# A decoder trunk on one core: the order of value products, the layout of the compression inputs, and a projection tile of 32 features

## The chip, the cores and the metric

The program runs on one core of one Trainium2 chip. The metric is the device time of one execution in microseconds (us). Engines: PE is the matrix engine (PEld its weight loads), DVE, ACT and POOL work on tiles, SP issues the DMAs. All five run their own instruction lists in order and wait for each other by semaphores.

## The reference

Two layers work on a stream x of 512 tokens by 1024 features. Layer 0 mixes tokens by sparse attention, layer 1 by an RWKV-7 recurrence; each adds attention into 256 memory tokens, an output projection and a gated FFN. All is float32. Three places matter here:

```
# layer 0, compression of keys and of values (kv: 512 tokens x 4 groups x 64)
idx = arange(31)[:, None] * 16 + arange(32)[None, :]
blocks = kv[:, idx] + pos                      # 31 blocks of 32 tokens, 16 apart
hid = gelu(einsum('bnlgd,lde->bnge', blocks, w1))   # w1: 32 places x 64 x 128
# layer 0, selected and window branch, per group of 3 heads
o_s = einsum('bgrqk,bgqkd->bqgrd', p_s, vg)    # probabilities times values, 64 wide
o_w = einsum('bgrqk,bkgd->bqgrd', p_w, vwc)
# memory attention, per head: p (512 x 256) times v (256 x 64)
# layer 1: one projection h @ w_in, of which the gate input has 160 columns
r, k, v, zw, za, zg = split(z, [768] * 3 + [64, 64, 160])
```

## The kernel before

Features lie on the 128 partitions and the 512 tokens along the row. A projection (`gemm`) makes a tile of 128 features: its weights are loaded as eight blocks of 128x128, and weights (`wsp`) and inputs (`nxh`/`nxl`, `wxh`/`wxl`, ...) are each split into a high and a low part, so a block takes three products in one PSUM tile `pm`: high by high, high by low, low by high (`mm3`). That makes 24 products of 512 columns a tile.

The program is first recorded as a list of operations (`Rec.add`). A planner (`Rec.schedule`) then sets the order: it steps through time with a cost per operation (`cost`), lets each engine take the ready operation that stands first in the recorded list (plus a bias for the projections that serve as filling), and keeps bounds on tiles alive. A matrix product that uses a part of the array (`colmode`) is joined to others of the same mode where one is ready. The order it finds is each engine's instruction list; the chip then keeps it. Every instruction is issued from line 517, so the profile tells them apart by tiles only.

The places that the change touches:

- **Attention of layer 0** (`nsa`): per group g of 3 heads and tile qt of 128 queries, probabilities `p` of two branches are transposed on PE (`ptr`), copied to `ap` by ACT or DVE, and multiplied with the values `vst`. The product of a branch is 64 wide: branch 0 writes partitions 0 to 63 of `po`, branch 1 partitions 64 to 127 (`tile_position=(0, 64 * br)`). There are 80 such products of 384 columns (float32, which is two PE instructions each). The memory attention (`mem_attn`, four times) does the same with its two heads, `mpt` and `mvs`, 512 columns, in `pa`.
- **Compression** (`compress`, once for keys, once for values): two projections give `kcf` (128 features, 512 tokens); SP copies them by DMA into `kc2`, 64 partitions at a time, the upper half shifted by one token. Then 16 float32 products with the weights `cw1` take every 16th column, 129 of them (32 blocks x 4 groups, and one column of the position vector `cpos`). The buffer `kc2` exists once.
- **Layer 1** (`rwkv`): tile 20 of the input projection holds the last 32 columns of the gate input, padded with zeros to 128, and is computed like every other tile. Only rows 0 to 31 of its result (`zg2`) are read.

Of the kernel before, what the change touches and what calls it, by code (L numbers as in the profile page):

```python
# [11 lines left out]
F32 = mybir.dt.float32  # L12
F32R = mybir.dt.float32r
F16 = mybir.dt.float16
AF = mybir.ActivationFunctionType
ALU = mybir.AluOpType
# [545 lines left out]
def cost(eng, meth, args, kw, outs, ins):  # L562

    def size(v):
        return int(np.prod(v.shape[1:])) if len(v.shape) > 1 else 1
    if meth == "dma_start":
        v = (outs + ins)[0]
        return v.shape[0] * size(v) * 4 / 350.0, 0
    n = max(size(v) for v in outs)
    ps = any(v.t.tag[1] for v in outs[:1] + ins)  # L570
    if eng == "tensor":
        if meth == "transpose":
            dt, m = ins[0].dt, outs[0].shape[0]
            return (0.85 if dt == F32 else 0.45) * size(ins[1]) * 1.0 + 2, 158
        w, x = ins[0], ins[1]
        m, n = w.shape[-1] if len(w.shape) == 2 else size(w), size(x)
        if x.dt == F32:
            t = n * 4 / 2.4 + 5
            if n == 129:
                t *= 2  # L580
            if m <= 64 and w.shape[0] <= 64:
                t = 58.0 if n <= 64 else 55.0
            elif n <= 64 and m <= 64:
                t = 54.0 if m > 32 else 27.0
            elif n >= 256 and m == 64:
                t = n * 2 / 2.4 + 5
            elif n < 128:
                t = max(t, 215.0 if m > 64 else 112.0 if m > 32 else 60.0)
        elif x.dt == F32R:
            t = n / 2.4 + 13  # L590
        else:
            t = n / 2.4 + 2 if m > 64 else 16
        return t, 158
    if eng == "vector":
        cols = [v for k, v in kw.items() if k.startswith("scalar") and isinstance(v, AV)]
        t = 67 + 61 * bool(cols)
        if meth == "reciprocal":
            return 67 + n * 8 / 1.2, 92
        if meth in ("tensor_reduce", "tensor_tensor_reduce"):
            n = size(ins[0])  # L600
            return t + n / 0.96 + 12, 92
        fast = meth in ("tensor_copy", "tensor_scalar", "memset") and not ps
        if meth == "tensor_tensor" and all(v.dt == F16 for v in outs + ins):
            fast = True
        return t + n / (1.92 if fast else 0.96), 92
    if eng == "scalar":
        t = (51 if ps else 93) + n * 0.833
        if isinstance(kw.get("scale"), AV):
            t += 93
        if "accum_out" in kw:  # L610
            t += 145
        return t, 110
    if meth == "tensor_tensor":
        return 150 + 2.1 * n, 40
    if meth == "memset":
        return 60 + 0.75 * n, 60
    return 250 + 0.77 * n, 40


class B:  # L620
# [203 lines left out]
                                                          scalar2=None, op0=ALU.mult)))  # L824

    def copied(self, out, ps):
        self.nc.flex(("scalar", "copy", (out, ps), {}), ("vector", "tensor_copy", (out, ps), {}))

    def kdup(self, kf, half, kh, kl):

# [18 lines left out]
    def mem_attn(self, m, qm, kv, ot):  # L849

        nc = self.nc
        kh, kl, vs = kv
        qs = [self.qstack(qm, i, "mqs") for i in range(2)]
        prs = []
        for qt in range(4):
            ps = self.ax_ps()
            tok = slice(qt * 128, qt * 128 + 128)
            for i in range(2):
                h = 2 * m + i
                o = ps[:, 256 * i:256 * i + 256]  # L860
                nc.tensor.matmul(o, qs[i][:, tok], kh[h], start=True, stop=False)
                nc.tensor.matmul(o, qs[i][:, tok], kl[h], start=False, stop=True)
            mn = self.sm("mmn", [128, 2], bufs=4)
            nc.vector.tensor_reduce(out=mn, in_=ps.rearrange("p (i n) -> p i n", i=2),
                                    op=ALU.min, axis=AX.X)
            sm = self.sm("msm", [128, 2], bufs=4)
            p = self.s2("mp")
            for i in range(2):
                nc.scalar.activation(p[:, 256 * i:256 * i + 256], ps[:, 256 * i:256 * i + 256],
                                     AF.Exp, bias=mn[:, i:i + 1], scale=-1.0,  # L870
                                     accum_out=sm[:, i:i + 1])
            rs = self.sm("mrs", [128, 2], bufs=4)
            nc.vector.reciprocal(out=rs, in_=sm)
            for i in range(2):
                nc.gpsimd.tensor_scalar(out=p[:, 256 * i:256 * i + 256],
                                        in0=p[:, 256 * i:256 * i + 256],
                                        scalar1=rs[:, i:i + 1], scalar2=1.0,
                                        op0=ALU.mult, op1=ALU.mult)
            prs.append(p)
        po = self.ax_ps()  # L880
        for mt in range(2):
            pts = []
            for i in range(2):
                pt = self.ax_ps()
                for qt in range(4):
                    nc.tensor.transpose(pt[:, qt * 128:qt * 128 + 128],
                                        prs[qt][:, 256 * i + 128 * mt:256 * i + 128 * mt + 128],
                                        self.ident)
                pts.append(self.s2("mpt"))
                self.copied(pts[i], pt)  # L890

            for i in range(2):
                nc.tensor.matmul(po[64 * i:64 * i + 64], vs[mt][:, 2 * m + i], pts[i],
                                 start=mt == 0, stop=mt == 1, tile_position=(0, 64 * i))
        self.copied(ot[6 + m], po)


# [64 lines left out]
    def nsa(self, xt):  # L962
# [37 lines left out]
        def compress(kvis):  # L1000

            for kvi in kvis:


                flat = nc.tile([128, 2080], F32, "kc2", "kc2", 1)
                kc2 = flat[:, 0:2048].rearrange("p (g n) -> p g n", g=4)
                cpos = self.sm("cpos", [128, 16])
                nc.sync.dma_start(cpos, self.a["cpos"][kvi])
                nc.gpsimd.tensor_scalar(out=flat[:, 2048:2080:2], in0=cpos, scalar1=1.0,
                                        scalar2=1.0, op0=ALU.mult, op1=ALU.mult)  # L1010
                for m in range(2):
                    with self.fill(GB[0]):
                        ps = self.gemm(W[2 * kvi + m], xs)
                    kcf = self.s2("kcf")
                    nc.vector.tensor_tensor(out=kcf, in0=ps, in1=R, op=ALU.mult)
                    for half in range(2):
                        hs = slice(64 * half, 64 * half + 64)
                        g = 2 * m + half
                        nc.sync.dma_start(kc2[0:64, g, :], kcf[hs])
                        nc.sync.dma_start(kc2[64:128, g, 0:511], kcf[hs, 1:512])  # L1020
                ps = self.ax_ps()
                for c in range(2):
                    cw = self.wraw(self.a["cw1"][kvi][:, c * 1024:c * 1024 + 1024])
                    for l in range(8):
                        ll = 8 * c + l
                        w = cw[:, l * 128:l * 128 + 128]
                        nc.tensor.matmul(ps[:, :129], w, flat[:, 2 * ll:2 * ll + 2049:16],
                                         start=ll == 0, stop=ll == 15)
                pb = self.sm("cpb", [128, 1])
                nc.vector.tensor_copy(pb, ps[:, 128:129])  # L1030
# [148 lines left out]
        for g in range(G):  # L1179
# [15 lines left out]
            for qt in range(4):  # L1195
# [8 lines left out]
                for br in range(2):  # L1204
# [21 lines left out]
                    for r in range(3):  # L1226
# [1 line left out]
                        nc.gpsimd.tensor_scalar(out=p, in0=p, scalar1=rs3[:, r:r + 1],  # L1228
                                                scalar2=gate[:, qt, gc:gc + 1],
                                                op0=ALU.mult, op1=ALU.mult)  # L1230
                aps = []
                for kt in range(qt + 1):
                    for br in range(2):
                        pt = self.ax_ps("ptr", F32, (128, 384))
# [1 line left out]
                            nc.tensor.transpose(pt[:, r * 128:r * 128 + 128],  # L1236
                                                pbr[br][r][:, kt * 128:kt * 128 + 128], self.ident)
                        aps.append(self.s2("ap")[:, :384])
                        self.copied(aps[-1], pt)

                for kt in range(qt + 1):
                    for br in range(2):
                        nc.tensor.matmul(po[64 * br:64 * br + 64], vst[kt][:, br, g],
                                         aps[2 * kt + br], start=kt == 0, stop=kt == qt,
                                         tile_position=(0, 64 * br))
                for m2 in sorted({(3 * g + r) // 2 for r in range(3)}):
                    if ot[m2] is None:
                        ot[m2] = self.s2("ot")
# [12 lines left out]
        return ot  # L1261


    def rwkv(self, xt):
        nc = self.nc
        xs = [self.split(xt[k], "wx", self.v("n1_1", k)) for k in range(KT)]
# [8 lines left out]
            return proj(wa, ma, na), proj(wb, mb, nb)  # L1275

        def proj_(wi, mix, name):
            ps = self.gemm(W[wi], xs)
            z = self.s2(name)
            if mix is None:  # L1280
                nc.vector.scalar_tensor_tensor(out=z, in0=ps, scalar=-0.125, in1=R,
                                               op0=ALU.mult, op1=ALU.mult)
                return z
            nc.vector.tensor_tensor(out=z, in0=ps, in1=R, op=ALU.mult)

            d = self.s2("zd")
            nc.scalar.activation(d, z, AF.Copy, scale=omu[:, mix:mix + 1])
            nc.vector.scalar_tensor_tensor(out=d[:, 1:512], in0=z[:, 0:511],
                                           scalar=self.v("mu", mix), in1=d[:, 1:512],
                                           op0=ALU.mult, op1=ALU.add)  # L1290
            return d

# [539 lines left out]
```

## Time and profile before

| | |
|---|---|
| median of 3 runs | 1453.22 us (1451.1 to 1454.13) |
| the profiled execution | 1453.28 us, its span 1451.5 us |
| PE busy | 1418.1 us, 98% of the span |
| PE at full clock | 0.993 of it on average |
| DVE / ACT / POOL busy | 57% / 45% / 9% |
| DMA | 28.5% of the engines' time on the one queue, 92 GB/s |

A busy time counts from the start of an instruction to its modelled end, and ends overlap the next starts on PE. What a PE instruction costs is therefore read as the distance from its start to the next start. In a timeline row with a count (x16) the first start stands in front, and the next row's start says when the group let go.

### The profile page before, as it was taken

How to read it: one execution, taken by the hardware profiler on the slowest of the kernel's cores; microseconds unless marked ns; L12 is line 12 of the kernel's file. 1: busy time of each engine (PE TensorE's matmuls, PEld its weight loads, DVE VectorE, ACT ScalarE, POOL GpSimd, SP SyncE). 2: the span in 40 equal slices, each digit the busy share in tenths (PEclk: the TensorE clock that was granted, in tenths of full speed). 3: DMA queues.
4: the chain of work that ended last, by engine and by line, in shares of the span. 5: the costliest groups of instructions: out<-in, count | busy, mean ns of one | idle time of the engine just before them, and what ended most of it. 6: DMA issues, size and time to landing. Idle time of an engine off the chain costs nothing.

```text
span 1451.5 us, 24917 instructions
## 1 busy us (share of the span) xinstructions
PE 1418.1 (98%) x9914; PEld 1131.7 (78%) x9914; DVE 834.2 (57%) x1735; ACT 656.4 (45%) x1443; POOL 125.8 (9%) x214
## 2 busy tenths in 40 slices
PE   9999999999999999999999999999899999999997
PEld 7867776778888888888777777866688888888886
DVE  7754478756444544544559968786474444434435
ACT  7654477644223432333546565684452323312314
POOL 0232125310000000000000010210000000000003
PEclk9999999999999999999999999999999999999998
DMA  7333522232233323223213011012232333322212
GB/s 251 109 83 102 154 65 80 96 109 91 80 120 102 122 96 102 93 97 115 97 62 103 24 54 53 12 50 89 75 102 80 109 102 101 101 89 86 88 58 74
DMA packets 50228, 133.39 MB, mean 92 GB/s; under 512 B 6208, under 2 KB 14784, under 8 KB 50112
## 3 DMA queue, kind: packets, MB, share of 16 engines
q1 hardware_dynamic: 50112, 131.80, 28.5%
q8 instruction: 78, 1.28, 0.4%
q14 instruction: 38, 0.31, 0.1%
HBM read 122.34 MB, written 4.19 MB: 87 GB/s over the span
## 4 chain that ended last, share of the span: by engine, by line
PE 87%; DVE 4%; ACT 3%; DMA 2%; issue 1%; POOL 1%; SPq 0%; ACTq 0%; POOLq 0%; DVEq 0%
PE pm L517 68%; PE pa L517 13%; PE po L517 2%; PE pv L517 2%; PE ptr L517 2%; PE py L517 1%; DVE gram L517 1%; POOL p L517 1%; ACT tm L517 1%; DMA bias<-bias 0%; PE pg L517 0%; ACT gyo L517 0%; SPq L517 0%; POOL mp L517 0%; ACT p L517 0%
## 5 line engine op out<-in xcount | busy, mean ns | idle before, releaser
L517 PE MATMUL pm<-fxh,wsp 128*128 128x512 f32 x1408 | 435.1, 389 | 0.0
L517 DVE TENSOR_TENSOR wsp<-wraw,wsp 128x512 fp32r<-128x512 f32 (+2 forms) x432 | 280.8, 663 | 63.7 <-ACT wsp L517 61.7
L517 PEld LDWEIGHTS pm<-fxh,wsp 128*128 128x128 f32 x1408 | 264.1, 188 | 54.7
L517 ACT CAST wsp<-wraw 128x512 fp32r<-128x512 f32 (+2 forms) x432 | 238.6, 592 | 96.7 <-DMA wraw<-w_fi 66.2
L517 PE MATMUL pm<-fxl,wsp 128*128 128x512 f32 x704 | 274.0, 389 | 0.0
L517 PE MATMUL pm<-hxh,wsp 128*128 128x512 f32 (+1 forms) x736 | 220.4, 380 | 0.0
L517 PEld LDWEIGHTS pm<-hxh,wsp 128*128 128x128 f32 x736 | 136.3, 188 | 26.2
L517 PEld LDWEIGHTS pm<-fxl,wsp 128*128 128x128 f32 x704 | 132.1, 188 | 27.4
L517 PE MATMUL pm<-hxl,wsp 128*128 128x512 f32 (+1 forms) x368 | 139.4, 380 | 0.0
L517 DVE TENSOR_TENSOR xt<-pm,xt 128x512 f32<-128x512 f32 (+1 forms) x80 | 50.4, 637 | 133.5 <-PE pm L517 133.3
L517 PE MATMUL pm<-wxh,wsp 128*128 128x512 f32 x368 | 126.1, 408 | 0.0
L517 ACT CAST hxh<-hu 128x512 fp32r<-128x512 f32 x44 | 27.3, 621 | 207.6 <-DVE hu L517 207.6
L517 DVE TENSOR_TENSOR hu<-pm,R 128x512 f32<-128x512 f32 x44 | 30.4, 692 | 121.6 <-PE pm L517 121.6
L517 ACT ACTIVATE hg<-hg 128x512 f32<-128x512 f32 x44 | 27.8, 632 | 153.4 <-DVE hg L517 153.4
L517 PE MATMUL pm<-oxh,wsp 128*128 128x512 f32 x256 | 86.8, 411 | 1.2 <-ACT mp L517 0.7
L517 PE MATMUL pm<-nxh,wsp 128*128 128x512 f32 x256 | 86.4, 405 | 1.6 <-ACT nxh L517 1.1
L517 POOL TENSOR_SCALAR p<-p,ars,gate 128x128 f32<-128x128 f32 (+3 forms) x96 | 72.0, 765 | 173.8 <-DVE ars L517 107.3
L517 PEld LDWEIGHTS pm<-wxh,wsp 128*128 128x128 f32 x368 | 67.4, 188 | 18.5 <-issue 5.8
L517 PEld LDWEIGHTS pm<-hxl,wsp 128*128 128x128 f32 x368 | 69.2, 188 | 13.1
L517 DVE TENSOR_TENSOR hg<-pm,R 128x512 f32<-128x512 f32 x44 | 30.4, 692 | 80.4 <-PE pm L517 75.5
L517 PE MATMUL pm<-wxl,wsp 128*128 128x512 f32 x184 | 74.6, 405 | 0.0
L517 ACT ACTIVATE p<-p,amn 128x128 f32<-128x128 f32 (+3 forms) x96 | 53.4, 559 | 19.4 <-DVE amn L517 18.9
(313 smaller groups left out, 2104.8 us busy)
## 6 DMA issues: line engine op xcount, KB each, us to landing
wraw<-w_fi SPq DMA_DIRECT2D x88, 512.0 KB, 3.3
wraw<-w_fo SPq DMA_DIRECT2D x24, 512.0 KB, 3.3
wraw<-w_rw SPq DMA_DIRECT2D x23, 512.0 KB, 3.4
wraw<-w_fo SPq DMA_DIRECT2D x24, 384.0 KB, 3.0
wraw<-w_o SPq DMA_DIRECT2D x16, 512.0 KB, 3.3
wraw<-w_nsa SPq DMA_DIRECT2D x12, 512.0 KB, 3.7
xt<-xT SPq DMA_DIRECT2D x16, 256.0 KB, 5.1
bias<-bias SPq DMA_DIRECT2D x12, 256.0 KB, 4.6
```

Source lines behind the costliest of these rows:

```text
L517: o.ret = getattr(getattr(nc, o.eng), o.meth)(*[res(x) for x in o.args], **{k: res(v) for k, v in o.kw.items()})
```

## The change

Three parts:

- **Value products in pairs.** `copied` returns its operation, and the product of each half names, for the planner alone, the copies of both halves as things to come after (`after=done`). No instruction is added.
- **Compression inputs by place.** `kc2` is now laid out as 8 places by 132 columns per partition: place l of a stride of 16 tokens, with odd and even tokens on the two partition halves, so that a product reads 130 neighbouring columns. The multiplication that makes `kcf` writes it sorted by place, reading `pm` and `R` 16 columns apart. A DMA moves 64 partitions with 8 pieces of 32 numbers each. POOL zeroes two columns and copies the positions in two steps. The planner's price for a product of 129 columns goes.
- **The 32-feature tile.** `narrow` copies the low parts of the 32 weight columns beside the high ones (ACT, two copies), so that one weight block holds both; two products a block are enough, 16 instead of 24. The result's rows 32 to 63 are then added to rows 0 to 31 (one ACT copy, one DVE addition), and what follows works on 32 partitions.

```diff
@@ cost
-            if n == 129:
-                t *= 2
@@ copied
-        self.nc.flex(("scalar", "copy", (out, ps), {}), ("vector", "tensor_copy", (out, ps), {}))
+        return self.nc.flex(("scalar", "copy", (out, ps), {}), ("vector", "tensor_copy", (out, ps), {}))
@@ mem_attn (nsa alike, with done[2 * kt:2 * kt + 2])
-                self.copied(pts[i], pt)
+                done.append(self.copied(pts[i], pt))
...
-                                 start=mt == 0, stop=mt == 1, tile_position=(0, 64 * i))
+                                 start=mt == 0, stop=mt == 1, tile_position=(0, 64 * i),
+                                 after=done)
@@ compress
-                flat = nc.tile([128, 2080], F32, "kc2", "kc2", 1)
-                kc2 = flat[:, 0:2048].rearrange("p (g n) -> p g n", g=4)
+                kc2 = nc.tile([128, 8, 132], F32, "kc2", "kc2", 1)
...
-                    nc.vector.tensor_tensor(out=kcf, in0=ps, in1=R, op=ALU.mult)
+                    k4 = kcf.rearrange("p (j e n) -> p j e n", j=8, e=2)
+                    def by_place(t):
+                        return t.rearrange("p (n j e) -> p j e n", j=8, e=2)
+                    nc.vector.tensor_tensor(out=k4, in0=by_place(ps), in1=by_place(R), op=ALU.mult)
...
-                        nc.sync.dma_start(kc2[0:64, g, :], kcf[hs])
-                        nc.sync.dma_start(kc2[64:128, g, 0:511], kcf[hs, 1:512])
+                        for e in range(2):
+                            nc.sync.dma_start(kc2[64 * e:64 * e + 64, :, 32 * g:32 * g + 32],
+                                              k4[hs, :, e, :])
...
-                        nc.tensor.matmul(ps[:, :129], w, flat[:, 2 * ll:2 * ll + 2049:16],
+                        nc.tensor.matmul(ps[:, :130], w, kc2[:, l, c:c + 130],
@@ new, for tile 20
+    def narrow(self, src, xs):
+        ps = self.mm_ps()
+        for c, (wh, wl) in enumerate(self.wload(src)):
+            w3, l3 = (w.rearrange("p (k n) -> p k n", k=4) for w in (wh, wl))
+            nc.scalar.copy(w3[:, :, 32:64], l3[:, :, 0:32])
+            for kk in range(4):
+                k, w = 4 * c + kk, wh[:, 128 * kk:128 * kk + 128]
+                nc.tensor.matmul(ps, w, xs[k][0], start=k == 0, stop=False)
+                nc.tensor.matmul(ps, w, xs[k][1], start=False, stop=k == KT - 1)
+        z = self.s2("zn")
+        nc.scalar.copy(z[0:32], ps[32:64])
+        nc.vector.tensor_tensor(out=z[0:32], in0=ps[0:32], in1=z[0:32], op=ALU.add)
```

How the order moves, in three places. PE, the first memory attention of layer 0 (`mpt` are its transposed probabilities; one row is one product, two PE instructions); before:

```order
L517 MATMUL pa<-cf,mp 128x128 x2
L517 MATMUL pa<-mpt,mvs 64x512
L517 MATMUL pa<-kl,qs 128x256
L517 MATMUL pa<-kh,qs 128x384
L517 MATMUL pa<-mpt,mvs 64x512 x3
L517 MATMUL ptr<-cf,p 128x128 x6
```

and of the changed program:

```order
L517 MATMUL pa<-kh,qs 128x384
L517 MATMUL pa<-kl,qs 128x384
L517 MATMUL pa<-kh,qs 128x384
L517 MATMUL pa<-kl,qs 128x384
L517 MATMUL pa<-mpt,mvs 64x512 x4
L517 MATMUL ptr<-cf,p 128x128 x6
```

One product stood alone and three in a row; now four stand in a row, the halves in turn.

PE, ahead of the products of the first compression (`kc` and a number is its input buffer), before:

```order
L517 MATMUL po<-ap,vst 64x384 x3
L517 MATMUL pm<-nxh,wsp 128x512
L517 MATMUL pm<-nxl,wsp 128x512
L517 MATMUL pm<-nxh,wsp 128x512 x2
L517 MATMUL pm<-nxl,wsp 128x512
L517 MATMUL pm<-nxh,wsp 128x512 x2
L517 MATMUL ptr<-cf,p 128x128 x3
L517 MATMUL pm<-nxl,wsp 128x512
L517 MATMUL ptr<-cf,p 128x128 x3
L517 MATMUL pm<-nxh,wsp 128x512
L517 MATMUL ptr<-cf,p 128x128
L517 MATMUL pa<-kc_1118,wraw 128x129 x16
```

and of the changed program:

```order
L517 MATMUL pa<-kh,qs 128x384
L517 MATMUL pa<-kl,qs 128x384
L517 MATMUL pa<-kh,qs 128x384
L517 MATMUL pa<-kl,qs 128x384
L517 MATMUL po<-ap,vst 64x384 x4
L517 MATMUL pm<-nxh,wsp 128x512
L517 MATMUL pa<-kc_67,wraw 128x130 x16
```

In both programs the last product of the projection that feeds `kcf` stands ahead of twelve products `pa<-kh,qs` and `pa<-kl,qs` of 384 columns, of which the four ahead of `po` are the last. Between it and the compression stand 31 products and transposes before, 17 after; at the second compression it is 34 before and 23 after, the first 23 alike.

SP, the DMAs of the second compression (`w_mk` and `w_mv` are weights of 512 KB each), before:

```order
L517 DMA kc_1604<-kcf 64x511
L517 DMA wraw<-w_mk 128x1024
L517 DMA kc_1604<-kcf 64x512
L517 DMA kc_1604<-kcf 64x511
L517 DMA wraw<-w_mv 128x1024
L517 DMA kc_1604<-kcf 64x512
L517 DMA kc_1604<-kcf 64x511
L517 DMA wraw<-w_mv 128x1024
```

and of the changed program:

```order
L517 DMA wraw<-w_mk 128x1024
L517 DMA kc_1584<-kcf 64x8x32 x4
L517 DMA wraw<-w_mk 128x1024
L517 DMA kc_1584<-kcf 64x8x32 x4
L517 DMA wraw<-w_mv 128x1024 x2
```

The last four copies now stand ahead of both loads of `w_mv`; before, one load stood among them.

## Rows read from the trace of the kernel before

**Rows 1.** The page: the span and the busy times (us, share of the span, instructions).

```profile
span 1451.5 us, 24917 instructions
...
PE 1418.1 (98%) x9914; PEld 1131.7 (78%) x9914; DVE 834.2 (57%) x1735; ACT 656.4 (45%) x1443; POOL 125.8 (9%) x214
```

**Rows 2.** Busy times in the stretch that holds layer 0's attention (stretch and its length in us, busy us and instructions of PE, PEld, DVE, ACT and POOL, PE clock, DMA share, GB/s).

```profile
0.00:290.00 290.00, 278.10 (x1540) 212.69 (x1540) 189.53 (x529) 185.70 (x493) 80.26 (x120) 1.00 0.39 118
```

**Rows 3.** What PE waited for (us in total, times, longest).

```profile
PE ptr L517 <- POOL p L517: 4.6, 5, 1.6
...
PE pa L517 <- DMA kc<-kcf: 0.8, 1, 0.8
```

**Rows 4.** PE's timeline at the two groups of compression products (start us, us, engine line op, out<-in, shape, count, idle time before and who ended it).

```profile
125.67 7.20 PE L517 MATMUL pa<-kc,wraw 128*128 128x129 f32 x32
132.70 1.38 PE L517 MATMUL ptr<-cf,p 128*128 128x128 f32 x11
...
161.97 7.26 PE L517 MATMUL pa<-kc,wraw 128*128 128x129 f32 x32 [0.84 <-DMA kc<-kcf]
168.88 0.82 PE L517 MATMUL pm<-nxh,wsp 128*128 128x512 f32 x2
```

**Rows 5.** PE's timeline at float32 products of 128 neighbouring columns (the sum of squares of the first norm).

```profile
28.21 1.05 PE L517 MATMUL pa<-cf,sq 128*128 128x128 f32 x8
29.02 0.48 PE L517 MATMUL pm<-nxh,wsp 128*128 128x512 f32 x1
```

**Rows 6.** PE's timeline at three groups of attention value products, each with the row after it, and the row ahead of the second and of it the next start.

```profile
82.34 4.08 PE L517 MATMUL po<-ap,vst 128*64 128x384 f32 x18
86.35 0.50 PE L517 MATMUL pa<-kh,qs 128*128 128x512 f32 x1
...
96.72 0.39 PE L517 MATMUL pm<-nxh,wsp 128*128 128x512 f32 x1
97.03 2.80 PE L517 MATMUL po<-ap,vst 128*64 128x384 f32 x16
99.77 0.50 PE L517 MATMUL pm<-nxh,wsp 128*128 128x512 f32 x1
...
189.11 0.86 PE L517 MATMUL po<-ap,vst 128*64 128x384 f32 x2
189.90 0.33 PE L517 MATMUL ptr<-cf,p 128*128 128x128 f32 x1
```

**Rows 7.** PE's timeline at the first memory attention's value products.

```profile
252.90 1.07 PE L517 MATMUL pa<-mpt,mvs 128*64 128x512 f32 x2
253.90 0.38 PE L517 MATMUL pa<-kl,qs 128*128 128x256 f32 x1
...
254.39 1.93 PE L517 MATMUL pa<-mpt,mvs 128*64 128x512 f32 x6
256.25 0.87 PE L517 MATMUL ptr<-cf,p 128*128 128x128 f32 x6
```

**Rows 8.** PE's timeline in layer 1's projections around tile 20: two rows between whose starts 24 products of 512 columns, as many as a tile has, were issued.

```profile
702.40 0.39 PE L517 MATMUL pm<-wxl,wsp 128*128 128x512 f32 x1
...
707.84 0.39 PE L517 MATMUL pm<-wxl,wsp 128*128 128x512 f32 x1
```

**Rows 9.** The timeline of all engines ahead of the first compression: the last product of its projection, the multiplication that makes `kcf`, the four DMAs, and what PE did meanwhile.

```profile
118.85 0.39 PE L517 MATMUL pm<-nxh,wsp 128*128 128x512 f32 x1
...
119.35 0.69 DVE L517 TENSOR_TENSOR kcf<-pm,R 128x512 f32<-128x512 f32 x1 [4.62 <-PE pm L517]
...
120.07 2.39 SPq L517 DMA_DIRECT2D kc<-kcf  x4
...
121.28 1.50 PE L517 MATMUL po<-ap,vst 128*64 128x384 f32 x6
...
122.71 0.50 PE L517 MATMUL pm<-nxh,wsp 128*128 128x512 f32 x1
...
123.05 0.40 PE L517 MATMUL pm<-nxl,wsp 128*128 128x512 f32 x1
```

**Rows 10.** The instructions that write or read `kcf` (duration in ns, least, median and most), and the time of their DMAs to landing.

```profile
L517 SPq DMA_DIRECT2D kc<-kcf x16: 461/594/957, 112.1 to 157.9; - x16
...
DMA to landing us min/median/max: 2.2/2.3/4.1
```

**Rows 11.** PE's timeline ahead of the second compression: the last product of its projection (first of the two), and the start at which 23 more had been issued.

```profile
154.37 0.71 PE L517 MATMUL pm<-nxh,wsp 128*128 128x512 f32 x2
...
158.57 0.27 PE L517 MATMUL ptr<-cf,p 128*128 128x128 f32 x1
```

**Rows 12.** SP's timeline there: a load of weights, and the last two copies of `kcf` behind it.

```profile
156.81 0.53 SPq L517 DMA_DIRECT2D wraw<-w_mv  x1
157.38 1.10 SPq L517 DMA_DIRECT2D kc<-kcf  x2
```

**Rows 13.** DMA issues (count, KB each, median us from issue to landing), and the page's row of the queue (packets, MB, share of 16 engines' span).

```profile
out<-xout SPq DMA_DIRECT2D x8, 256.0 KB, 2.4
...
kc<-kcf SPq DMA_DIRECT2D x8, 128.0 KB, 2.3
mkh<-mkh SPq DMA_DIRECT2D x16, 64.0 KB, 1.9
...
q1 hardware_dynamic: 50112, 131.80, 28.5%
```

More of the change, by code (lines that the diff above doesn't have):

```diff
@@ L881, in mem_attn @@
         for mt in range(2):
-            pts = []
+            pts, done = [], []
             for i in range(2):
@@ L1002, in compress @@
             for kvi in kvis:
-                flat = nc.tile([128, 2080], F32, "kc2", "kc2", 1)
-                kc2 = flat[:, 0:2048].rearrange("p (g n) -> p g n", g=4)
+                kc2 = nc.tile([128, 8, 132], F32, "kc2", "kc2", 1)
                 cpos = self.sm("cpos", [128, 16])
                 nc.sync.dma_start(cpos, self.a["cpos"][kvi])
-                nc.gpsimd.tensor_scalar(out=flat[:, 2048:2080:2], in0=cpos, scalar1=1.0,
-                                        scalar2=1.0, op0=ALU.mult, op1=ALU.mult)
+                nc.gpsimd.memset(kc2[:, :, 130:132], 0.0)
+                for j in range(2):
+                    nc.gpsimd.tensor_scalar(out=kc2[:, :, 128 + j], in0=cpos[:, 8 * j:8 * j + 8],
+                                            scalar1=1.0, scalar2=1.0, op0=ALU.mult, op1=ALU.mult)
                 for m in range(2):
@@ L1230, in nsa @@
                                                 op0=ALU.mult, op1=ALU.mult)
-                aps = []
+                aps, done = [], []
                 for kt in range(qt + 1):
@@ L1238, in nsa @@
                         aps.append(self.s2("ap")[:, :384])
-                        self.copied(aps[-1], pt)
+                        done.append(self.copied(aps[-1], pt))
                 for kt in range(qt + 1):
@@ L1244, in nsa @@
                                          aps[2 * kt + br], start=kt == 0, stop=kt == qt,
-                                         tile_position=(0, 64 * br))
+                                         tile_position=(0, 64 * br),
+                                         after=done[2 * kt:2 * kt + 2])
                 for m2 in sorted({(3 * g + r) // 2 for r in range(3)}):
@@ L1261, in nsa @@
         return ot
+    def narrow(self, src, xs):
+        nc = self.nc
+        ps = self.mm_ps()
[9 more added lines that the diff above has]
+        nc.vector.tensor_tensor(out=z[0:32], in0=ps[0:32], in1=z[0:32], op=ALU.add)
+        return z[0:32]
     def rwkv(self, xt):
@@ L1277, in proj_ @@
         def proj_(wi, mix, name):
-            ps = self.gemm(W[wi], xs)
-            z = self.s2(name)
+            ps = self.narrow(W[wi], xs) if wi == 20 else self.gemm(W[wi], xs)
+            hs = slice(0, 32 if wi == 20 else 128)
+            z = self.s2(name)[hs]
             if mix is None:
@@ L1283, in proj_ @@
                 return z
-            nc.vector.tensor_tensor(out=z, in0=ps, in1=R, op=ALU.mult)
-            d = self.s2("zd")
-            nc.scalar.activation(d, z, AF.Copy, scale=omu[:, mix:mix + 1])
+            nc.vector.tensor_tensor(out=z, in0=ps, in1=R[hs], op=ALU.mult)
+            d = self.s2("zd")[hs]
+            nc.scalar.activation(d, z, AF.Copy, scale=omu[hs, mix:mix + 1])
             nc.vector.scalar_tensor_tensor(out=d[:, 1:512], in0=z[:, 0:511],
-                                           scalar=self.v("mu", mix), in1=d[:, 1:512],
+                                           scalar=self.v("mu", mix)[hs], in1=d[:, 1:512],
                                            op0=ALU.mult, op1=ALU.add)
```

## The prediction

> **What bounds the kernel now.** I read the page first: PE is busy for 1418.1 of 1451.5 us [rows 1], so the order and the length of PE's own instructions set the time, and work on another engine counts only where PE waits for it. The stretch with layer 0's attention, where two of the three parts lie, is the same picture: 278.1 of 290 us, at full clock [rows 2]. Next the waits: PE waited for the compression's DMA once, for 0.84 us, and five times for POOL's probabilities, 4.6 us together [rows 3]; that is what an earlier PE can run into. Then the timeline, for the distance from a start to the next, since busy times overlap. What the reader is to see there: compression products cost double, value products cost by how they stand in the order, projections run without a gap.
>
> **Compression by place, on PE.** The two groups of 32 instructions last 132.70 - 125.67 = 7.03 and 168.88 - 161.97 = 6.91 us [rows 4], 13.94 us, 0.218 each for 129 columns. Eight float32 instructions over 128 neighbouring columns, each with its own weight load as here, took 29.02 - 28.21 = 0.81 us, 0.101 each [rows 5]; the last of a group is partly hidden, so I take 0.11 for 130 columns: 64 x 0.11 = 7.0. **Gain 6.9 us.** Nothing gained would be the other bound (if the double length were not the stride); the shapes differ in little else, so I stay by rows 5.
>
> **Compression by place, ahead of PE.** This is the price. The chain before: last product of the projection at 118.85, `kcf` on DVE from 119.35 for 0.69, four DMAs from 120.07 that take 2.39 to issue [rows 9], so the last goes out about 0.6 earlier than 122.46 (median issue 594 ns), at 121.87, and lands 2.3 later [rows 10]: 124.2, which is 5.3 us behind the last product. PE had 31 operations to put between and reached the products only at 125.67 [rows 4], later than the data. Now 17 stand between. At the old lengths twelve products of 384 columns reach to 121.28, a group of four `po` products in pairs takes as long as the three there (1.43, to 122.71), one more projection product 0.34, to 123.05 [rows 9]: cover 123.05 - 118.85 = 4.2 us. So even with the old DMAs PE would wait 5.3 - 4.2 = 1.1 us. The second compression is the same: the 23 operations that remain reach from 154.37 to 158.57, 4.2 us [rows 11]. Its chain had been longer because a load of 512 KB was issued among its copies [rows 12], after which they took up to 4.1 us to land [rows 10]; in the new order of SP that load stands behind them, so I use 5.3 here too.
>
> What the new chain adds is not in the trace. First, a copy of 64 pieces of 2 KB becomes one of 512 pieces of 128 B. By bytes it halves, and a copy of 64 KB in 64 pieces landed in 1.9 us, 0.4 sooner than these [rows 13]: lower bound -0.4. The output's copies, 256 pieces of 1 KB and 256 KB, landed in 2.4: 0.5 us for 192 pieces and 192 KB more than the 64 KB copy. If all of that is by the piece, 448 more pieces cost 1.2 us, and four such copies behind each other, issued 0.6 apart, pile up to about 3 us on the last: upper bound +3. I take +0.75, near the copies that the trace has, since those 0.5 us also carry bytes. Second, `kcf`'s multiplication reads 16 columns apart; between no loss and a doubling (as PE's strided products in rows 4 against rows 5) lie 0 and +0.7, and I take +0.35, since no row of DVE shows such a stride. So PE waits 1.1 + 1.1 = 2.2 us twice, 4.4, and the old wait of 0.84 goes: **loss 3.6 us.** Behind a waiting product stand PE's whole list, and all engines that it feeds.
>
> The Trainium skill (DMA: Bandwidth & Descriptors) speaks on both sides of this. Its Specifications say that pieces under 512 B lose line rate by a read and a write back; its section "Why small descriptors are slow (HBM only)" says that copies within the on-chip memory do not suffer from that. By the first a 64 KB copy would count as 256 KB, an estimate near my +0.75; by the second near -0.4. No row here has such pieces.
>
> **Value products in pairs.** Two instructions of different halves run side by side: the group of 16 lasts 99.77 - 97.03 = 2.74, the group of two 189.90 - 189.11 = 0.79 [rows 6]. So a group costs 0.79 plus (2.74 - 0.79) / 3 = 0.65 for each further step, a step being one product or a pair of neighbours of different halves. The group of 18 (nine products) checks this: 86.35 - 82.34 = 4.01 is 0.79 + 5 x 0.65, six steps, so only three of its nine products found a partner. Counted over the order, with the half that each product writes, the 80 products made 47 steps in 18 groups before; now 43 in 16 (the first tiles of group 0, which still wait for the second branch's values, keep theirs apart). With 0.145 a group, that is 0.79 - 0.65, 4 x 0.65 + 2 x 0.145 = 2.9 us. The memory attention had one product alone and three in a row: 253.90 - 252.90 = 1.00 and 256.25 - 254.39 = 1.86 [rows 7]. Four in turn are two steps, as the three were, so 1.00 us goes each time; of the four calls one was paired already: 3.0 us. Entering such a group costs once more: the product ahead of one lasts 97.03 - 96.72 = 0.31, where the stream has 0.227, and five entries go: 0.4. **Gain 6.3 us.** The price would be PE waiting for a partner's copy; the order puts other products between, so I see none of its own.
>
> **The 32-feature tile.** 24 products take 707.84 - 702.40 = 5.44 us, 0.227 each [rows 8]; eight go. **Gain 1.8 us.** The two copies on ACT and what follows for `zg2` lie beside PE: ACT is busy for 45% [rows 1], weights are split ahead, and the result is first read by a product much later. If the copies came late, PE would wait for well under a microsecond, the length of one of them.
>
> **The rest.** PE runs through 290 us some 13 us sooner, and POOL, ACT and DVE don't. The 4.6 us of waits for POOL [rows 3] show where it would meet them; between nothing and another 4.6 I take a third, **loss 1.5 us**. In layer 1 the order shifts by a few places around the eight products, of either sign; I put nothing.
>
> **The sum.** 6.9 + 6.3 + 1.8 = 15.0 of gain, 3.6 + 1.5 = 5.1 of loss: 9.9 us off the profiled execution's 1453.28, which is 0.06 above the median. Forecast 1443.4.
>
> **The rivals.**
> - *The copies are in time.* If small pieces land like the 64 KB copies and the stride costs DVE nothing, the wait is about 0.7 twice, little more than what goes, and with no loss elsewhere: 1453.3 - 15.0 + 0.6 = 1438.9. For it speaks that the bytes halve and that the load leaves the queue's way; against it, that the cover shrank from 31 operations to 17.
> - *The pieces are dear but bounded.* With +3 for the copies and +0.7 for DVE the wait is 4.8 twice, 9.6 - 0.84 = 8.8 lost, and with 1.5 elsewhere 1448.6; 4.6 elsewhere makes it 1451.7.
> - *Slower than before.* A packet of this program takes 0.285 x 16 x 1451.5 / 50112 = 0.132 us of an engine on average [rows 13]. If a piece of 128 B cost as much, each copy would hold its engine for 32 x 0.132 = 4.2 us, four of them 16.9; with 1.9 to land, PE would wait about 0.5 + 0.7 + 18.8 - 4.2 = 15.8 twice, which makes 1453.3 - 15.0 - 0.8 + 31.6 + 1.5 = 1470.6. It decides from about 0.07 us a piece: there four copies last 9 us, and the two waits eat the 15 us. Against it: those packets carry 2.6 KB on average, and the output's 256 pieces land in 2.4 us.
> - *The pairs do not pay.* If the half products already overlapped as the planner left them, or copies come too late for both, the 6.3 goes: 1449.7. Rows 6 and 7 speak against it.
>
> **How the numbers follow.** Forecast (1440.5 to 1447) 0.66; copies in time 0.15; dear but bounded 0.10; slower 0.03; pairs don't pay 0.06. What this measurement can tell from no change is 0.2%, 2.9 us, so faster is below 1450.3. The first two cases are faster, most of the third and of the last too: 0.66 + 0.15 + 0.06 + 0.03 = 0.90; of the 0.10 left 0.06 lies within 0.2% and 0.04 is slower. The range is 1437 to 1450: it takes in the copies in time and the bounded price, and leaves out the ends of both.
>
> **What would show it.** The two groups of 32 should last about 3.5 us each. A wait of PE for `kc<-kcf` of 1 to 4 us should stand ahead of each; landing times of `kc<-kcf` and the length of `kcf` on DVE tell which part was dear. The `mpt` groups should show eight instructions in 1.86 us, and `po` 160 in about 30. Sixteen products should make tile 20. New waits for `p` or `ap` below 290 us would be the 1.5. I am wrong if the groups of 32 keep their 7 us, if the copies wait over 5 us, or if waits in layer 1 grow by more than 3 us.

## The result and the profile after

The changed kernel takes 1438.59 us (median of 4 runs, 1437.14 to 1439.5) against 1452.99 (4 runs): ratio 0.9906 [0.9892, 0.9921], 14.4 us less. On a second chip it was 1437.79 against 1452.49, ratio 0.99 [0.9882, 0.9917], with the same 3.1 us of waits for `kc<-kcf` as below. The forecast was 1443.4: right in sign and inside its range, 4.8 us too high, and the time lies below the band of 1440.5 to 1447 that had the chance of 0.66. The profiled execution took 1438.80.

The page of the changed kernel and what PE waited for in it answer to [rows 1, 3]:

```profile
span 1437.0 us, 24900 instructions
PE 1402.7 (98%) x9906; PEld 1122.5 (78%) x9906; DVE 835.1 (58%) x1734; ACT 659.0 (46%) x1448; POOL 124.6 (9%) x218
```

```profile
PE pa L517 <- DMA kc<-kcf: 3.1, 2, 1.6
PE ptr L517 <- POOL p L517: 2.1, 5, 1.2
```

PE is as full as before with 15.4 us less to do. The wait for the compression's copies, once 0.8 us, is now 3.1 in two places; the wait for POOL halved, where I had expected it to grow.

PE's timeline at the compressions [rows 4, 9], the first memory attention [rows 7] and tile 20 [rows 8]:

```profile
121.51 1.51 PE L517 MATMUL po<-ap,vst 128*64 128x384 f32 x8
122.95 0.49 PE L517 MATMUL pm<-nxh,wsp 128*128 128x512 f32 x1
124.94 3.81 PE L517 MATMUL pa<-kc,wraw 128*128 128x130 f32 x32 [1.49 <-DMA kc<-kcf]
128.59 2.13 PE L517 MATMUL ptr<-cf,p 128*128 128x128 f32 x18
...
157.56 3.81 PE L517 MATMUL pa<-kc,wraw 128*128 128x130 f32 x32 [1.61 <-DMA kc<-kcf]
161.21 0.27 PE L517 MATMUL ptr<-cf,p 128*128 128x128 f32 x1
...
244.63 1.94 PE L517 MATMUL pa<-mpt,mvs 128*64 128x512 f32 x8
246.50 0.88 PE L517 MATMUL ptr<-cf,p 128*128 128x128 f32 x6
...
693.82 0.39 PE L517 MATMUL pm<-wxh,wsp 128*128 128x512 f32 x1
...
697.22 0.39 PE L517 MATMUL pm<-wxl,wsp 128*128 128x512 f32 x1
697.45 0.62 PE L517 MATMUL pm<-wxh,wsp 128*128 128x512 f32 x2
```

A compression now lasts 128.59 - 124.94 = 3.65 us where it lasted 7.03, the memory products 1.87 in one group where there were 2.86 in two, and tile 20 697.45 - 693.82 = 3.63 where a tile takes 5.44. All engines ahead of the first compression, and the instructions on `kcf` [rows 9, 10]:

```profile
119.09 0.39 PE L517 MATMUL pm<-nxh,wsp 128*128 128x512 f32 x1
119.51 1.05 DVE L517 TENSOR_TENSOR kcf<-pm,R 128x512 f32<-128x512 f32 x1 [2.37 <-PE pm L517]
120.59 2.63 SPq L517 DMA_DIRECT2D kc<-kcf  x4
```

```profile
L517 SPq DMA_DIRECT2D kc<-kcf x16: 591/633/1688, 111.7 to 155.2; - x16
L517 DVE TENSOR_TENSOR kcf<-pm,R x4: 1042/1056/1065, 110.6 to 152.1; 128x512 f32<-128x512 f32 x4
DMA to landing us min/median/max: 2.1/2.3/3.8
```

The chain from the last product to the compression is 124.94 - 119.09 = 5.85 us; PE's own work covers 5.85 - 1.49 = 4.36 of it. The copies land after a median of 2.3 us, as they did with pieces of 2 KB.

The fall of PE's span can be shared out by the distance from each start to the next, with the idle time before an instruction kept apart (sums over all instructions of a tile, before to after). Half clock is time in which PE was granted 1.2 GHz instead of 2.4; what it cost is an estimate:

| | us | |
|---|---|---|
| compression products | -6.64 | 13.94 to 7.29 |
| `po` and `mpt` products | -5.96 | 33.05 to 30.22, 10.59 to 7.47 |
| layer 1's input projection | -1.94 | eight products fewer |
| waits for `kc<-kcf` | +2.26 | 0.84 to 3.10 |
| all other waits of PE, those for POOL among them | -1.73 | 25.15 to 23.42 |
| transposes of `p`, products with `kh` and `mkh` | +2.1 | 1.10 + 0.55 + 0.46 |
| half clock | -3.3 | 5.72 to 2.44: busy time times (1 - granted clock), over stretches of 1 us |
| what is left | +0.7 | the span fell by 14.48 |

Whether the half clock is the change's doing is open: it differs as much between executions of one kernel, but 1.7 us of it may hang on a wait that the new order shortens (last section). Without it the change takes 11.2 us from this pair of executions.

### The profile page after: what moved, and what is told of

Read it like the earlier page. It is cut to its first block, busy times and chain, and to the rows that moved or that the text cites. A ratio compares the mean times of both kernels' runs of the same rounds, so it can differ in the third digit from the quotient of the medians.

```text
span 1437.0 us, 24900 instructions
## 1 busy us (share of the span) xinstructions
PE 1402.7 (98%) x9906; PEld 1122.5 (78%) x9906; DVE 835.1 (58%) x1734; ACT 659.0 (46%) x1448; POOL 124.6 (9%) x218
## 4 chain that ended last, share of the span: by engine, by line
PE 88%; DVE 4%; ACT 3%; DMA 1%; issue 1%; POOL 1%; SPq 0%; ACTq 0%; POOLq 0%; DVEq 0%
PE pm L517 69%; PE pa L517 12%; PE po L517 2%; PE pv L517 2%; PE ptr L517 2%; PE py L517 1%; POOL p L517 1%; DVE gram L517 1%; DMA kl<-kl 1%; ACT gyo L517 1%; ACT tm L517 0%; PE pg L517 0%; POOL mp L517 0%; SPq L517 0%; DMA kc<-kcf 0%
## 5 line engine op out<-in xcount | busy, mean ns | idle before, releaser
L517 POOL TENSOR_SCALAR p<-p,ars,gate 128x128 f32<-128x128 f32 (+3 forms) x96 | 68.9, 733 | 171.9 <-DVE ars L517 105.3
```

Source lines behind the costliest of these rows:

```text
L517: o.ret = getattr(getattr(nc, o.eng), o.meth)(*[res(x) for x in o.args], **{k: res(v) for k, v in o.kw.items()})
```

## The experiments

**Each part alone.** Each is the kernel before with one part of the change. The pairs (`copied`, `mem_attn`, `nsa`):

```diff
+                done.append(self.copied(pts[i], pt))
...
+                                 after=done)
```

> The value products in pairs alone, the rest as before. Theory (the parts add, each worth what its own groups of PE lose): the po products fall from 33.1 to about 30.2 us, the memory attention's from 10.6 to 7.5, and the time by 6.0 to 6.5 us, to about 1446.6. Rival (part of the 14.4 us is owed to a lucky new order, or the parts hold each other up): the groups fall as said, but the time falls by under 4 or over 8 us, and the waits of PE, not its groups, make the difference.

The compression (`cost`, `compress`):

```diff
-                        nc.tensor.matmul(ps[:, :129], w, flat[:, 2 * ll:2 * ll + 2049:16],
+                        nc.tensor.matmul(ps[:, :130], w, kc2[:, l, c:c + 130],
```

> The compression by place alone (with the planner's price for 129 columns gone). Theory: the two groups of 32 last 7.3 us together instead of 13.9, PE waits 3 us instead of 0.8 for the copies, and the time falls by about 4.4 us, to 1448.6. Rival (the wait for the copies is bought back elsewhere, as PE's other waits fell by 1.7 us in the whole change): it falls by 6 us or more. Rival (the wait delays what follows): by under 3.

The 32-feature tile (`narrow` and its call):

```diff
-            ps = self.gemm(W[wi], xs)
+            ps = self.narrow(W[wi], xs) if wi == 20 else self.gemm(W[wi], xs)
```

> The 32-feature tile alone. Theory: eight products of 0.227 us go, and the time falls by 1.8 us, to 1451.2. Rival (the eight products were filling under waits of layer 1, which then show): it falls by under 0.9 us, and PE's waits in layer 1 grow.

Measured on one chip (before there 1451.27): pairs 1444.34, ratio 0.9955 [0.9942, 0.9969]; compression 1442.70, 0.994 [0.9924, 0.9955]; tile 1451.01, 0.9992 [0.9979, 1.0004]. The pairs hold: `po` 30.22 and `mpt` 7.47 us in the trace, as in the whole change, so the 5.96 is theirs. The tile's trace has the 1.8 us in its products, and PE's longest waits in layer 1 are as before (`lth` 2.8, `gyo` 2.4, `ry` 1.7), but its time cannot be told from none. The compression alone fell by 8.6 us, about twice the 4.4 of the theory, and beyond the 6 of the first rival. In its profiled execution the 64 products and the wait came as in the whole change. The order that the planner finds for it also puts some value products in pairs (`mpt` -1.00, `po` -0.61), PE's other waits fell by 1.3, as that rival has it, and half clock cost 2.3 us less than in the profiled execution of before; the clock of one execution says nothing of the median. The three ratios add up to 1.1%, where the whole change has 0.9 to 1.0: 1.6 us is in two of them, and each is uncertain by 0.1 to 0.2%.

**Stride or odd count.** The compression products changed from 129 columns 16 apart to 130 side by side. One kernel is the changed one with 129 side by side, the other the kernel before with 130 columns 16 apart (one column of zeros more).

```diff
-                        nc.tensor.matmul(ps[:, :130], w, kc2[:, l, c:c + 130],
+                        nc.tensor.matmul(ps[:, :129], w, kc2[:, l, c:c + 129],
...
-                        nc.tensor.matmul(ps[:, :129], w, flat[:, 2 * ll:2 * ll + 2049:16],
+                        nc.tensor.matmul(ps[:, :130], w, flat[:, 2 * ll:2 * ll + 2065:16],
```

> The changed kernel with 129 instead of 130 neighbouring columns a product. Theory (the stride of 16 columns made the old products twice as long): an instruction stays at about 0.11 us and the two groups at 7.2 to 7.3 us. Rival (an odd number of columns did, as the planner's old price for 129 had it): they go back to 0.22 us each and 13.9 us, and the time rises by 6 us or more.

> The kernel before with 130 instead of 129 columns a product, still 16 apart. Theory (the stride): 0.22 us an instruction, the groups at 13.9 to 14.1 us, the time as before. Rival (the odd number): 0.11 us, 7.2 us, and the time 6 us below that of before.

The instructions on `kc`, first side by side, then 16 apart (ns, least, median, most):

```profile
L517 PE MATMUL pa<-kc,wraw x64: 275/275/348, 124.4 to 160.6; 128*128 128x129 f32 x64
```

```profile
L517 PE MATMUL pa<-kc,wraw x64: 397/398/440, 126.8 to 169.2; 128*128 128x130 f32 x64
```

From start to start the 64 take 7.29 and 14.07 us (the kernels, one execution each, 1439.26 and 1450.74; before on that chip 1452.47). The price is that of columns 16 apart; other strides were not tried.

**Where `kcf`'s multiplication pays.** It reads two tiles 16 columns apart and writes in order; here it reads in order and writes 32 columns apart.

```diff
-                    nc.vector.tensor_tensor(out=k4, in0=by_place(ps), in1=by_place(R), op=ALU.mult)
+                    nc.vector.tensor_tensor(out=kcf.rearrange("p (j e n) -> p n j e", j=8, e=2),
+                                            in0=ps.rearrange("p (n j e) -> p n j e", j=8, e=2),
+                                            in1=R.rearrange("p (n j e) -> p n j e", j=8, e=2),
+                                            op=ALU.mult)
```

> The changed kernel, with the multiplication that makes kcf reading its two inputs in order and writing 32 columns apart, instead of reading 16 apart and writing in order. Theory (the reading apart costs the 0.36 us): kcf takes 0.69 us again, the wait ahead of the compression falls by 0.36 twice, and the time by about 0.7 us. Rival (any stride costs the same, wherever it stands): kcf stays at 1.05 us and nothing changes. A third way (writing apart is dearer): over 1.2 us, and the wait grows.

```profile
L517 DVE TENSOR_TENSOR kcf<-pm,R x4: 1090/1106/1124, 112.4 to 154.0; 128x512 f32<-128x512 f32 x4
```

The plain multiplication takes 0.69 us [rows 9]; with both inputs 16 apart it was 1.06, with the output 32 apart 1.11. The theory falls: DVE pays on either side, and the time stayed (1438.38, ratio 0.9897 [0.9881, 0.9914]).

**Halves not in turn.** To test that two products run together only as neighbours of different halves, one branch's `po` products all stand ahead of the other's.

```diff
-                for kt in range(qt + 1):
-                    for br in range(2):
+                for br in range(2):
+                    for kt in range(qt + 1):
...
-                                         after=done[2 * kt:2 * kt + 2])
+                                         after=done)
```

> The changed kernel with the attention's value products of one half ahead of all of the other half, so that neighbours mostly write the same half. Theory (only neighbours of different halves run side by side, 0.646 us a step and 0.145 a group): 66 steps instead of 43, the po products rise from 30.2 to 45 us, the time by 14 to 15 us, to about 1453. Rival (the halves overlap through PE's queue wherever they stand in a group): po stays near 30 us and the time within 2 us of 1438.6.

It took 1445.23 us (one execution), and `po` 39.52 in all, 38.9 without the idle time in it: neither 45 nor 30. Its groups, with the rows behind them:

```profile
123.68 1.52 PE L517 MATMUL po<-ap,vst 128*64 128x384 f32 x8
125.13 0.49 PE L517 MATMUL pm<-nxh,wsp 128*128 128x512 f32 x1
...
134.23 2.80 PE L517 MATMUL po<-ap,vst 128*64 128x384 f32 x12
136.96 0.50 PE L517 MATMUL pm<-nxh,wsp 128*128 128x512 f32 x1
...
168.43 4.14 PE L517 MATMUL po<-ap,vst 128*64 128x384 f32 x16
172.50 0.73 PE L517 MATMUL pm<-nxh,wsp 128*128 128x512 f32 x2
```

The last is four products of one half and then four of the other, AAAABBBB: 4.07 us, which by 0.79 and 0.65 a further step is six steps. Neighbours alone would make seven, halves in turn four. AAABBB (the group of 12) took 2.73, four steps instead of five, and AABB (the group of 8) 1.45, two instead of three. All three follow if each half has one product running and one more waiting, and only a third holds up those behind it: AAABBB then runs as A, AB, AB, B, and AAAABBBB as A, A, AB, AB, B, B. The starts in the trace agree: of the 16 instructions of AAAABBBB the first four start one at a time, 0.32 to 0.37 us apart, the next eight in four pairs whose starts are at most 0.06 us apart, and the last four one at a time again. Counted so, this order has 56 steps, 38.6 us against the 38.9 measured; the kernel before keeps its 47 steps (33.07, measured 33.05) and the changed one 43 (30.19, measured 30.22). My count of neighbours is a special case that fits those two. How a half comes to hold a second product is inferred from these durations and starts, not shown.

**The wait.** Did it come from the planner's ignorance? It reckons a copy into `kc2` by its bytes, and `kcf`'s multiplication as one of the plain kind. This is the changed kernel with two prices:

```diff
+        if v.t.name == "kc2":
+            return 600.0, 0
...
-        t = 67 + 61 * bool(cols)
+        t = 67 + 61 * bool(cols) + 360 * (outs[0].t.name == "kcf")
```

> The changed kernel, with the planner's prices for the four copies (600 ns each) and for the multiplication that makes kcf (360 ns more) as the trace of the changed kernel shows them. Theory (the wait ahead of the compression stands there because the planner thinks the copies land 1.8 us sooner than they do): the planner puts other products between, PE's wait for kc<-kcf falls from 3.1 us to under 0.5, and the time by 2 to 3 us, to about 1436. Rival (PE's waits only move: what is drawn forward is missing later): the wait for the copies falls as said, other waits grow by as much, and the time stays within 1 us of 1438.6.

> The changed kernel with two prices told to the planner (600 ns for a copy into kc2, 360 more for kcf's multiplication), beside the changed kernel on one chip. Theory 'the wait is a cover that the planner leaves short because it takes the copies for short': no wait for kc<-kcf, idle time of PE some 1.6 us less (24.9 against 26.5) as in the first look at it, and a time 2 to 4 us below the changed kernel's. Rival 'the wait only moves': PE waits as long elsewhere, and the two medians agree within 1 us.

First 1435.19 us, ratio 0.9894 [0.9875, 0.9914], with 24.9 us of idle time of PE; then, beside the changed kernel's 1437.79, 1436.58 with 0.9887 [0.9871, 0.9902]. PE's timeline in the second, and its longest waits:

```profile
122.48 0.50 PE L517 MATMUL pm<-nxh,wsp 128*128 128x512 f32 x1
122.82 0.40 PE L517 MATMUL pm<-nxl,wsp 128*128 128x512 f32 x1
123.06 0.62 PE L517 MATMUL pm<-nxh,wsp 128*128 128x512 f32 x2
123.52 0.39 PE L517 MATMUL pm<-nxl,wsp 128*128 128x512 f32 x1
123.75 0.62 PE L517 MATMUL pm<-nxh,wsp 128*128 128x512 f32 x2
124.20 0.49 PE L517 MATMUL ptr<-cf,p 128*128 128x128 f32 x3
124.45 0.48 PE L517 MATMUL pm<-nxl,wsp 128*128 128x512 f32 x1
124.77 3.73 PE L517 MATMUL pa<-kc,wraw 128*128 128x130 f32 x32
```

```profile
PE ptr L517 <- POOL p L517: 5.1, 8, 1.3
PE pg L517 <- ACT gyo L517: 2.4, 1, 2.4
```

The compression starts at 124.77 with no idle time before it, and seven more products of the projections and three transposes stand ahead. The wait was a cover that the planner left short. But most of what is gained comes back as 5.1 us for `p`, 3.0 more than in the changed kernel: PE's idle time falls only from 26.2 (changed kernel, beside it) to 25.4. The time fell by 1.2, between what the theory and the rival had named, and no more than one kernel's executions differ. I then gave the planner the trace's durations for POOL's work on `p` too, with the two prices and without:

```diff
+    if outs[0].t.name == "p":
+        return {128: 515.0, 256: 650.0, 384: 660.0, 512: 1006.0}[n], 40
```

> The version with the two prices for the compression, and the planner's price for POOL's work on p set to what the trace shows (515, 650, 660 and 1006 ns for 128, 256, 384 and 512 columns, where it reckoned 348 to 644). Theory 'PE's waits in layer 0 are covers that the planner leaves short because a price is low': the waits for p, 5.1 us in 8 places there, fall under 2 us, no wait for kc<-kcf appears, the idle time of PE falls from 25.4 to about 22 us and the time by 2 to 3 us, to some 1433.5. Rival 'layer 0 runs out of work that could stand in the waits': the waits only change their names, idle time stays at 25 us and the time within 1 us.

> The changed kernel with the price of p alone. Theory of low prices: the 3.1 us for kc<-kcf stay, the 2.1 for p go below 1, idle time about 25.2 against 26.2 to 26.5, time 1 us below the changed kernel's. Rival: the same 26 us under other names, and the time unchanged.

With both 1434.94 (0.9883 [0.9863, 0.9903]), with `p`'s price alone 1436.15 (0.9894 [0.9875, 0.9914]); before 1450.89. What PE waited for with both, and with `p`'s alone:

```profile
PE ptr L517 <- POOL p L517: 3.4, 4, 1.7
PE pa L517 <- DMA kl<-kl: 2.5, 3, 1.6
...
PE ptr L517 <- DVE ap L517: 1.3, 1, 1.3
```

```profile
PE pa L517 <- DMA kc<-kcf: 3.1, 2, 1.6
...
PE ptr L517 <- POOL p L517: 1.2, 2, 0.6
```

The theory of low prices falls for the sum: idle time is 26.6 and 25.8 us, where 22 and 25.2 were expected. The waits change their names, as the rival said. The versions with prices stand 1 to 4 us below the changed kernel, which ran beside only one of them: too little to be told apart here. They beat the kernel before.

## Why the prediction was right, point by point

- **Compression on PE, -6.9: right.** -6.64; 3.65 us a group. That the stride is the cause, which I took from two shapes that differ in little else, is shown by the pair of 129 and 130.
- **The wait, +3.6: right in kind, too big.** It measured +2.26, 1.49 and 1.61 us a time instead of 2.2. The cover was right (4.36 for 4.2). Of the terms added to the chain, the stride's +0.35 on DVE came as +0.36, but the +0.75 for small pieces, the term that was mis-sized, had no counterpart: the last copy of each compression landed after 2.15 us (2.30 before at the first, 3.95 at the second, behind the load), and only the issue of the four grew, 2.63 for 2.39. In all the chain is 5.85, not 6.4. By the rows below, 512 pieces took 2.3 us at the median, 64 pieces with the same bytes 2.0. The 0.3 us over 28 more pieces an engine is an estimate of 0.011 us a piece, and the trace's packets of 128 B took 0.012 each, so the slower rival's 0.07 was far off. The Trainium skill (DMA: Bandwidth & Descriptors) had spoken on both sides; by its section "Why small descriptors are slow (HBM only)", copies within the chip do not suffer. The trace agrees as far as these 0.3 us go.

```profile
kc<-kcf SPq DMA_DIRECT2D x16, 64.0 KB, 2.3
mkh<-mkh SPq DMA_DIRECT2D x16, 64.0 KB, 2.0
```

- **Pairs, -6.3: right.** -2.84 and -3.12 in the products, shown by the part alone. The 0.4 for five entries did not appear. Instead PE's transposes and key products cost 2.1 us more in the new order, a price for which the prediction has no term; what in the order costs it was not tried.
- **The 32-feature tile, -1.8: right** in the trace (-1.94, and -1.83 alone); no time could confirm it.
- **The rest, +1.5: the wrong step.** I let PE run into POOL's probabilities. Those waits fell from 4.6 to 2.1, all waits but the compression's by 1.73, and the transposes and key products gave 2.1 back: +0.4 net. The wait for `lth`, a tile of layer 1, fell from 2.8 to 1.3 with the pairs alone and stayed at 2.8 with the compression or the tile alone, so the order that the planner finds with the pairs brings that part.
- **What no term held: the clock.** 3.3 us of the 14.5 between the two profiled executions is half clock.

So the 4.6 us by which the profiled execution beat the forecast are 1.3 of wait, 1.1 of the rest and 3.3 of clock, less 1.2 on the products, their entries and what is left. The rival with the copies in time named 1438.9, but by another way: it had the waits at 0.7 us, and they are twice that. That the time comes so near to that rival's is luck.

## What to carry to other kernels

When an edit shortens the instructions that stand between a producer's chain and its consumer, work out the cover and the chain from the timeline; that gave the new wait to within 0.7 us a time here. A wait bought back in a full order is not gained until the engine's whole idle time falls: compare that sum, not the row that vanished. And look at the granted clock of both profiled executions before a difference of a few microseconds is given to an edit.

## What was not expected of the hardware

Executions of one kernel on one chip differ by up to 7 us, and the mean granted clock goes with it: beside all these kernels, the one before took 1452.5 to 1456.1 in 16 executions at 0.993 and 1449.9 to 1452.0 in 7 at 0.997. Of the changed kernel's ten executions one had 0.993. Stretches of 5 us in layer 1 show where: the kernel before, and the one with the compression alone (stretch and length, PE busy, granted clock, DMA share, GB/s).

```profile
1045.00:1050.00 5.00, 1.21 (x7) 0.95 0.01 2
1050.00:1055.00 5.00, 4.69 (x11) 0.50 0.00 0
1055.00:1060.00 5.00, 5.00 (x20) 0.87 0.33 105
```

```profile
1037.00:1042.00 5.00, 0.90 (x6) 1.00 0.00 0
1042.00:1047.00 5.00, 5.00 (x16) 0.66 0.09 30
```

Both had just waited 1.7 us for `ry` and 2.4 for `gyo`; after that PE ran at 1.2 GHz for a time, which cost about 3.0 us in the first and 1.7 in the second (busy time times the missing share of the clock). What decides how long was not tried.

The kernel before has a second such stretch, the compression alone too. In the kernel before, PE had waited 1.50 us for `lth` until 986.92. The rows are PE's timeline there, the stretches around it, and the waits for `lth` before and in the changed kernel:

```profile
986.92 0.31 PE L517 MATMUL pa<-chh,lth 64*64 64x64 f16 x8 [1.50 <-DVE lth L517]
```

```profile
983.00:988.00 5.00, 3.50 (x29) 1.00 0.00 0
988.00:993.00 5.00, 5.00 (x43) 0.66 0.00 0
```

```profile
PE pa L517 <- DVE lth L517: 2.8, 4, 1.5
```

```profile
PE pa L517 <- DVE lth L517: 1.3, 3, 0.8
```

The stretch cost 1.7 us. Four traced kernels have this wait of 1.5 us (before, the compression alone, the tile alone, 130 columns 16 apart), and two of them a stretch at half clock behind it. In the ten traces with the pairs the longest wait for `lth` is 0.8 us, and none has a stretch at half clock there. So the pairs may also have bought clock; one trace a kernel does not show it.

Two more. A half of the array seems to take a second product ahead (above). And 512 columns took DVE about 0.4 us longer with its two inputs 16 columns apart or its output 32 apart; other strides were not tried.
